# First latent step queued ahead of the second intra-chunk group, fewer late sums in the scan, direction sums on GpSimd

## Chip, core and metric

One core of a Trainium2 chip runs the whole program once. The number that counts is the device time of one execution in microseconds (us), median over the runs; lower is better. Five engines take part, each with a queue of its own that is worked off in order: TensorE (PE; its weight loads are shown apart as PEld), VectorE (DVE), ScalarE (ACT), GpSimd (POOL) and SyncE (SP), which issues the DMAs.

## What is computed

One layer of a diffusion backbone: 512 latent tokens and 256 context tokens of width 1024. The part that the change touches is the gated delta rule, run over chunks of 64 tokens, forward and backward, with the state S (64x64 for each of 8 heads) carried from chunk to chunk:

```python
def step(S, xs):
    w_c, uv_c, qd_c, intra_c, kt_c, gl_c = xs
    u = uv_c - einsum('bhck,bhkv->bhcv', w_c, S)
    o = einsum('bhck,bhkv->bhcv', qd_c, S) + einsum('bhij,bhjv->bhiv', intra_c, u)
    S = exp(gl_c)[..., None, None] * S + einsum('bhck,bhcv->bhkv', kt_c, u)
    return S, o
...
o_dc, s_cf, s_cb = bidir_delta(context, zero, zero)
o_dl, _, _ = bidir_delta(latents, s_cf, s_cb)      # o_f + flip(o_b)
y_d = rms_norm(o_dl, dn_norm_g) * silu(z)
y = sigmoid(gate_a) * (y_a @ w_br_attn) + sigmoid(gate_d) * (y_d @ w_br_dn)
x = x + gt1 * (y @ w_out);  x = x + gt2 * mlp(x, sh2, sc2)
```

Here `intra_c` is the masked product of queries and keys inside a chunk (the intra-chunk matrices). `gt1`, `sh2`, `sc2`, `gt2` are sums over a 1024x6144 matrix times a vector; the kernel forms those four as late sums, since they are needed late.

## The kernel before

**Matmuls.** Large projections are three fp32 matmuls per 128x128 weight tile (high part times high, high times low, low times high). A weight tile is fetched by DMA into one of four buffers (`wfetch`, L250, tag `wr`), its high part made by ACT (L259, `wh`) and its low part by DVE (L262, `wl`); of `wh` and `wl` there are two buffers each.

**Fill.** The scan is a chain of short steps, so other matmuls are laid between them. `filler` is a generator over the attention branch's output and the gate tiles; `gate_tiles` (L1004) yields after each 128x512 matmul, 24 to a tile. A finished tile goes through an activation (L148 is the helper's line) and for some tiles a DVE operation (L1009).

**Late sums.** `late_mod` fetches 512 KB (L1068, into the same four `wr` buffers under the name `wa`) and multiplies and sums it on DVE (L1070, 128x1024). One call of `run_late` takes one such piece, so the buffer that it uses comes back when L1070 is done.

**Intra-chunk matrices.** Two groups g = 0, 1. Of each, PE forms query-key products (`half_products`, L754, two halves), with fill before and between (`run_both`, 24 fills counting 12 before and 12 between; it takes one late sum for every `LATE` fills). DVE then multiplies by decay masks (L1254, L1255) and copies (L1261), ACT copies (L1262, L1263) and GpSimd sets zeros (L1264, L1265).

**The scan over latents.** `steps(range(NCC, NC_))` walks 8 steps; in each, both directions go through three phases. Phase one: PE forms Z from keys, queries and the state (L1128), DVE forms R (L1132, L1133). Phase two: PE forms U (L1140), DVE scales it (L1146, `uk`), ACT copies it (L1150, `us`) and scales the query part (L1152, `zq`). Phase three: PE forms the state update (L1161) and the outputs inside the chunk (L1165); ACT decays the old state (L1175) and DVE subtracts (L1177), which is the state that the next Z needs. In the first four steps DVE adds the two output parts (L1184). In the last four the other direction has already written the place: DVE adds the parts (L1187), adds the sum to what stands there (L1189), ACT squares (L1190) and DVE reduces (L1191). After the three phases 8, 7 and 3 fills are taken, and a late sum after every third.

**What sets the order.** The code only gives the order in which the operations are recorded. A list scheduler then sets each engine's queue from its own cost estimates, so an engine's order can differ from the order of the code; a queue, once set, is worked off strictly in order.

Of the kernel before, what the change touches and what calls it, by code (L numbers as in the profile page):

```python
# [12 lines left out]
ALU = mybir.AluOpType  # L13
# [13 lines left out]
WARM = 3, 6, 4, 4  # L27
NONES = 16
AHEAD = 2
LATE = 12  # L30
HPAUSE = 2
FPAUSE, CPAUSE = 12, 16
NPL = ()
# [13 lines left out]
NCC = CTX // CH  # L47
NCL = SEQ // CH
NC_ = NCC + NCL
# [50 lines left out]
def tile_layer(ctx: ExitStack, tc: tile.TileContext, I: dict, out: bass.AP, dbg=None):  # L100
    nc = tc.nc
    V, A, G, PE = nc.vector, nc.scalar, nc.gpsimd, nc.tensor
# [26 lines left out]
    def dump(key, ap):  # L129
        if dbg is not None and key in dbg:  # L130
            nc.sync.dma_start(out=dbg[key], in_=ap)
# [532 lines left out]
    for src, cols in ((abx, slice(0, SEQ)), (abc, slice(SEQ, TOK))):  # L664
        n = cols.stop - cols.start
# [433 lines left out]
    def run_both(n):  # L1099

        for _ in range(n):
            next(fill, None)
            both[0] += 1
            if both[0] % LATE == 0:
                run_late(1)
# [8 lines left out]
    def chain_step(d, step):  # L1114
# [65 lines left out]
        if lat:  # L1180
            us.free()
            dst = ot_[:, cl * 256:(cl + 1) * 256]
            if step - NCC < NCL // 2:
                V.tensor_tensor(dst, zq, oi[:, :256], op=ALU.add)  # L1184
                oi.free()
            else:
                V.tensor_tensor(zq, zq, oi[:, :256], op=ALU.add)  # L1187
                oi.free()
                V.tensor_tensor(dst, dst, zq, op=ALU.add)  # L1189
                A.activation(zq, dst, AF.Square)  # L1190
                V.tensor_reduce(oss[:, cl], hv(zq), axis=AX.X, op=ALU.add)  # L1191
            zqb.free()

    def steps(r):
        for step in r:
            both = [chain_step(d, step) for d in range(2)]
            for _ in range(3):
                for g in both:
                    next(g, None)
                yield  # L1200
# [40 lines left out]
        b.free()  # L1241

    IA = [alloc(2048, True), alloc(2048, True)]
    ia = [v64(b.ap) for b in IA]
    for g in range(2):
        ms = slice(16 * g, 16 * g + 16)
        es = slice(512 * g, 512 * g + 512)
        run_both(FILL[2] - FPAUSE)
        qq_ = bank(2)
        qD, qO = diag_off(qq_)  # L1250
        for _ in half_products(qq_, 1 + g, qT):
# [13 lines left out]
            G.memset(ia[1][lo, ms, HC:], 0.0)  # L1265
    for b in ED + [EO]:
        b.free()
    dump("kT0", kT[0].ap)
    dump("qT0", qT[0].ap)

    ot_ = alloc(2048, True)
    ot = ot_.ap.rearrange("p (c q v) -> p c q v", c=NCL, q=4)
    for n, _ in enumerate(steps(range(NCC, NC_))):
        run_fill(FILL[3][n % 3])
        if n % 3 == 2:
            run_late(1)
    for _ in fill:
        pass
# [284 lines left out]
```

## Time and profile before

| | us |
|---|---|
| median of 3 runs | 921.29 |
| lowest, highest | 921.2, 923.67 |
| the profiled execution's own time | 922.56 |
| span of the profiled execution | 920.4 |
| mean granted clock, share of full | 0.994 |

The profile is of one execution. Its span runs from the first to the last instruction; 2.16 us of its time lie outside. Its time is 1.27 us above the median. A busy share of an engine is an average over the whole program; the stretch that the change touches lies between 385 and 485 us of the span: the two groups of query-key products, then the eight steps of the latent scan, then the rest of the fill. The rows below give, for stretches and single instructions, when an engine worked, how long it stood idle, and what ended the wait.

### The profile page before, as it was taken

How to read it: one execution, taken by the hardware profiler on the slowest of the kernel's cores; microseconds unless marked ns; L12 is line 12 of the kernel's file. 1: busy time of each engine (PE TensorE's matmuls, PEld its weight loads, DVE VectorE, ACT ScalarE, POOL GpSimd, SP SyncE). 2: the span in 40 equal slices, each digit the busy share in tenths (PEclk: the TensorE clock that was granted, in tenths of full speed). 3: DMA queues.
4: the chain of work that ended last, by engine and by line, in shares of the span. 5: the costliest groups of instructions: out<-in, count | busy, mean ns of one | idle time of the engine just before them, and what ended most of it. 6: DMA issues, size and time to landing. Idle time of an engine off the chain costs nothing.

```text
span 920.4 us, 16843 instructions
## 1 busy us (share of the span) xinstructions
PE 885.5 (96%) x7082; PEld 708.7 (77%) x7082; DVE 600.8 (65%) x1029; ACT 442.7 (48%) x821; POOL 12.9 (1%) x26
## 2 busy tenths in 40 slices
PE   7999998999899999979999999999999999999998
PEld 5668767867677678767778789888888888888886
DVE  3588898997787898567766978961563245324511
ACT  5577653357568886456664444650343035213400
POOL 0000000000000001010000000000000000000000
PEclk9999998999999999999999999999999999999999
DMA  9650112110000132533324674660443224322111
GB/s 353 254 201 1 47 47 69 47 47 24 24 13 24 55 105 85 182 119 94 114 61 175 220 249 130 219 210 23 160 137 92 69 92 137 100 71 83 45 46 46
DMA packets 28443, 98.24 MB, mean 107 GB/s; under 512 B 3536, under 2 KB 4176, under 8 KB 27344
## 3 DMA queue, kind: packets, MB, share of 16 engines
q1 hardware_dynamic: 28368, 97.18, 32.2%
q8 instruction: 55, 0.90, 0.4%
q14 instruction: 20, 0.16, 0.1%
HBM read 95.07 MB, written 2.10 MB: 106 GB/s over the span
## 4 chain that ended last, share of the span: by engine, by line
PE 78%; DVE 11%; ACT 5%; DMA 3%; issue 2%; SPq 0%; DVEq 0%; ACTq 0%
PE banks L315 18%; PE banks L313 18%; PE banks L314 18%; PE banks L1004 8%; PE banks L1049 2%; DMA wa<-in_wada 2%; DVE wl L262 1%; PE banks L571 1%; PE banks L1140 1%; PE banks L577 1%; PE banks L639 1%; PE banks L1161 1%; PE banks L578 1%; DVE m L1070 1%; DMA m<-in_xT 1%
## 5 line engine op out<-in xcount | busy, mean ns | idle before, releaser
L313 PE MATMUL banks<-m,m 128*128 128x512 f32 (+1 forms) x600 | 223.5, 377 | 2.8 <-DVE m L620 1.9
L314 PE MATMUL banks<-m,m 128*128 128x512 f32 (+1 forms) x600 | 224.5, 376 | 0.1
L315 PE MATMUL banks<-m,m 128*128 128x512 f32 (+1 forms) x600 | 224.5, 376 | 0.0
L259 ACT ACTIVATE m<-wr 128x1024 fp32r<-128x1024 f32 x68 | 71.7, 1059 | 151.6 <-PE banks L314 79.0
L313 PEld LDWEIGHTS banks<-m,m 128*128 128x128 f32 x600 | 111.9, 188 | 25.4 <-ACT m L319 2.5
L314 PEld LDWEIGHTS banks<-m,m 128*128 128x128 f32 x600 | 112.5, 188 | 22.1 <-DVE m L320 1.5
L315 PEld LDWEIGHTS banks<-m,m 128*128 128x128 f32 x600 | 112.5, 188 | 21.3 <-issue 1.2
L262 DVE TENSOR_TENSOR m<-wr,m 128x1024 fp32r<-128x1024 f32 x68 | 83.1, 1224 | 66.9 <-PE banks L314 34.2
L1004 PE MATMUL banks<-m,wh 128*128 128x512 f32 x320 | 105.0, 406 | 1.6 <-issue 1.1
L313 PE MATMUL banks<-m,wh 128*128 128x512 f32 (+1 forms) x280 | 103.8, 372 | 1.5 <-DVE m L595 1.0
L315 PE MATMUL banks<-m,wl 128*128 128x512 f32 (+1 forms) x280 | 101.6, 365 | 3.1 <-DVE wl L262 3.1
L314 PE MATMUL banks<-m,wh 128*128 128x512 f32 (+1 forms) x280 | 102.6, 367 | 0.0
L1447 DVE SCALAR_TENSOR_TENSOR m<-banks,modT,m 128x512 f32<-128x512 f32 x32 | 24.0, 750 | 101.2 <-PE banks L315 101.2
L259 ACT ACTIVATE wh<-wr 128x1024 fp32r<-128x1024 f32 (+1 forms) x58 | 54.5, 940 | 46.6 <-PE banks L314 19.5
L262 DVE TENSOR_TENSOR wl<-wr,wh 128x1024 fp32r<-128x1024 f32 (+1 forms) x58 | 62.2, 1073 | 18.8 <-ACT wh L259 18.8
L1004 PEld LDWEIGHTS banks<-m,wh 128*128 128x128 f32 x320 | 58.2, 189 | 14.4 <-issue 0.9
L1004 PE MATMUL banks<-m,wl 128*128 128x512 f32 x160 | 64.5, 403 | 0.0
L315 PEld LDWEIGHTS banks<-m,wl 128*128 128x128 f32 x280 | 53.3, 192 | 11.7 <-DVE wl L262 3.9
L313 PEld LDWEIGHTS banks<-m,wh 128*128 128x128 f32 x280 | 53.6, 192 | 10.1 <-DVE m L595 1.3
L314 PEld LDWEIGHTS banks<-m,wh 128*128 128x128 f32 x280 | 53.5, 191 | 8.2 <-issue 1.0
L184 ACT ACTIVATE m<-m 128x512 fp32r<-128x512 f32 (+1 forms) x56 | 34.8, 629 | 48.6 <-DVE m L1430 21.6
L1070 DVE SCALAR_TENSOR_TENSOR m<-wa,m 128x1024 f32<-128x1024 f32 x32 | 38.9, 1222 | 19.4 <-DMA wa<-in_wada 14.4
(237 smaller groups left out, 1266.3 us busy)
## 6 DMA issues: line engine op xcount, KB each, us to landing
wr<-in_wm SPq DMA_DIRECT2D x64, 512.0 KB, 3.7
wr<-in_win SPq DMA_DIRECT2D x38, 512.0 KB, 3.6
wa<-in_wada SPq DMA_DIRECT2D x32, 512.0 KB, 4.1
m<-in_wada SPq DMA_DIRECT2D x8, 1024.0 KB, 11.7
m<-in_xT SPq DMA_DIRECT2D x8, 512.0 KB, 5.9
wr<-in_wbr SPq DMA_DIRECT2D x16, 256.0 KB, 2.6
wr<-in_wout SPq DMA_DIRECT2D x8, 512.0 KB, 4.5
out<-m SPq DMA_DIRECT2D x8, 256.0 KB, 2.0
```

Of the source, the lines that this page charges most:

```text
L184: A.activation(r32(hi), src, AF.Copy)
L259: h = A.activation(r32(hi), raw, AF.Copy)
L262: V.tensor_tensor(r32(lo), raw, hi, op=ALU.subtract)
L313: PE.matmul(acc, w[0][:, k, :], xhi, start=(start and i == 0), stop=False)
L314: PE.matmul(acc, w[0][:, k, :], xlo, start=False, stop=False)
L315: PE.matmul(acc, w[1][:, k, :], xhi, start=False, stop=(stop and i == n - 1))
L571: PE.transpose(pt[:, j * P:(j + 1) * P], probs[j][:, i * P:(i + 1) * P], ident)
L577: PE.matmul(pv.ap, v, r32(phi), start=(i == 0), stop=False)
L1004: PE.matmul(acc.ap, w[x][:, k, :], hx[k][y], start=(k == p == 0), stop=(k == KT - 1 and p == 2))
L1049: PE.matmul(pa.ap, w[x][:, j, :], r32(Q[y][:, :, j, :]), start=(j == p == 0), stop=(j == 3 and p == 2))
L1070: V.scalar_tensor_tensor(t.ap, wa, 0.5, scr.ap, op0=ALU.mult, op1=ALU.mult, accum_out=modT[:, grp, j:j + 1])
L1447: V.scalar_tensor_tensor(xn_[ct], acc.ap, modT[:, 3, ct:ct + 1], xn_[ct], op0=ALU.mult, op1=ALU.add)
```

## The change

Four edits. `LATE` goes from 12 to 8: over the two groups' 72 fills nine late sums are taken in place of six. The first phase of the first latent step (Z and R of both directions) is recorded after the second group's first fills and ahead of its query-key products; the scan then goes on from its second phase, and 8 of the scan's fills fall to after its end. In the scan a late sum is taken after every third phase of the first four steps alone, so 13 have been taken by its end where 14 had been. The add of L1189 moves from DVE (`V`) to GpSimd (`G`): eight adds of 128x256.

```diff
-LATE = 12
+LATE = 8
...
-                V.tensor_tensor(dst, dst, zq, op=ALU.add)
+                G.tensor_tensor(dst, dst, zq, op=ALU.add)
...
     IA = [alloc(2048, True), alloc(2048, True)]
+    scan = steps(range(NCC, NC_))
     ia = [v64(b.ap) for b in IA]
     for g in range(2):
...
         run_both(FILL[2] - FPAUSE)
+        if g:
+            next(scan)
         qq_ = bank(2)
         qD, qO = diag_off(qq_)
         for _ in half_products(qq_, 1 + g, qT):
...
+    ot_ = alloc(2048, True)
     dump("kT0", kT[0].ap)
     dump("qT0", qT[0].ap)
 
-    ot_ = alloc(2048, True)
-    ot = ot_.ap.rearrange("p (c q v) -> p c q v", c=NCL, q=4)
-    for n, _ in enumerate(steps(range(NCC, NC_))):
+    for n, _ in enumerate(scan, 1):
         run_fill(FILL[3][n % 3])
-        if n % 3 == 2:
+        if n % 3 == 2 and n < 3 * NCL // 2:
             run_late(1)
```

What the scheduler makes of it is shown at three places. Behind L1243 the changed kernel's lines are higher by 1 to 3 (the masks L1254 and L1255 are L1257 and L1258, the copies L1261 are L1264).

PE, before: the end of the second group's second product, and behind it the first Z (`m_80` to `m_83` are the keys, `m_181`, `m_203`, `m_218`, `m_238` the queries, `m_273` a state, `banks` accumulators).

```order
L754 MATMUL banks_64<-m_203_2197,m_81_556 32x64 x4
L754 MATMUL banks_64<-m_218_2367,m_82_557 32x64 x4
L754 MATMUL banks_64<-m_238_2573,m_83_558 32x64 x4
L1128 MATMUL banks_64<-m_273_2825,m_80_555 64x64 x2
L1128 MATMUL banks_64<-m_273_2825,m_181_1868 64x64 x2
```

PE, now: the end of the first Z (`m_275` is the other direction's state), and behind it the second group's first product.

```order
L1128 MATMUL banks_64<-m_275_2827,m_82_557 64x64 x2
L1128 MATMUL banks_64<-m_275_2827,m_218_2367 64x64 x2
L1128 MATMUL banks_64<-m_275_2827,m_83_558 64x64 x2
L1128 MATMUL banks_64<-m_275_2827,m_238_2573 64x64 x2
L754 MATMUL banks_64<-m_181_1868,m_80_555 32x64 x4
L754 MATMUL banks_64<-m_203_2197,m_81_556 32x64 x4
```

The Z of both directions moved from behind the group's two products to ahead of them; the U that follows R now stands right behind the second product, with 15 fills after it, where 13 fills stood between Z and U.

DVE, before, at the same place: the last of the second group's copies, then R, then the first `uk`.

```order
L1261 COPY m_366_3885<-m_366_3885 32x16x32
L1261 COPY m_367_3886<-m_367_3886 32x16x32
L1132 TENSOR_TENSOR m_393_4185<-banks_64,eg_737 128x256
L1132 TENSOR_TENSOR m_394_4204<-banks_64,eg_737 128x256
L1133 SCALAR_TENSOR_TENSOR m_393_4185<-m_315_3144,m_393_4185 128x256
L1133 SCALAR_TENSOR_TENSOR m_394_4204<-m_322_3217,m_394_4204 128x256
L1009 SCALAR_TENSOR_TENSOR m_325_3260<-m_395_4207,m_325_3260 128x512
L1146 TENSOR_TENSOR m_399_4232<-banks_64,eg_737 128x256
```

DVE, now: behind the first group's copies come a weight split, a late sum, a gate tile's operation, and R; then a weight split and the second group's masks and copies.

```order
L262 TENSOR_TENSOR wl_391_4062<-wr_389_4059,wh_390_4061 128x1024
L1070 SCALAR_TENSOR_TENSOR m_414_4321,modT_2818<-wa_413_4319,m_346_3489 128x1024
L1009 SCALAR_TENSOR_TENSOR m_318_3197<-m_388_4056,m_318_3197 128x512
L1132 TENSOR_TENSOR m_394_4097<-banks_64,eg_737 128x256
L1132 TENSOR_TENSOR m_395_4116<-banks_64,eg_737 128x256
L1133 SCALAR_TENSOR_TENSOR m_394_4097<-m_315_3144,m_394_4097 128x256
L1133 SCALAR_TENSOR_TENSOR m_395_4116<-m_322_3217,m_395_4116 128x256
L262 TENSOR_TENSOR wl_410_4260<-wr_408_4257,wh_409_4259 128x1024
L1257 TENSOR_TENSOR m_366_3885<-m_90_757,banks_64 128x16x32
L1257 TENSOR_TENSOR m_367_3886<-m_91_758,banks_64 128x16x32
L1258 TENSOR_TENSOR m_92_759<-m_92_759,banks_64 128x512
```

R moved from behind the second group's masks and copies to ahead of them; the first `uk` (L1146) now stands behind these, and a late sum stands ahead of R.

DVE, before, at the change from the fifth step to the sixth: new states, sums of both directions, a late sum, and R.

```order
L1177 TENSOR_TENSOR m_272_2824<-m_468_4872,banks_64 128x256
L1187 TENSOR_TENSOR m_464_4826<-m_464_4826,banks_64 128x256
L1189 TENSOR_TENSOR m_392_4168<-m_392_4168,m_464_4826 128x256
L1177 TENSOR_TENSOR m_274_2826<-m_469_4898,banks_64 128x256
L1187 TENSOR_TENSOR m_467_4843<-m_467_4843,banks_64 128x256
L1191 TENSOR_REDUCE oss_271_2823<-m_464_4826 128x4
L1189 TENSOR_TENSOR m_392_4168<-m_392_4168,m_467_4843 128x256
L1070 SCALAR_TENSOR_TENSOR m_488_5069,modT_2818<-wa_487_5067,m_346_3489 128x1024
L1191 TENSOR_REDUCE oss_271_2823<-m_467_4843 128x4
L1132 TENSOR_TENSOR m_472_4931<-banks_64,eg_737 128x256
```

DVE, now, at the same place.

```order
L1177 TENSOR_TENSOR m_272_2824<-m_474_4876,banks_64 128x256
L1187 TENSOR_TENSOR m_465_4820<-m_465_4820,banks_64 128x256
L1177 TENSOR_TENSOR m_274_2826<-m_475_4902,banks_64 128x256
L1191 TENSOR_REDUCE oss_271_2823<-m_465_4820 128x4
L1187 TENSOR_TENSOR m_468_4837<-m_468_4837,banks_64 128x256
L1132 TENSOR_TENSOR m_476_4931<-banks_64,eg_737 128x256
L1191 TENSOR_REDUCE oss_271_2823<-m_468_4837 128x4
L1133 SCALAR_TENSOR_TENSOR m_476_4931<-m_322_3217,m_476_4931 128x256
L1132 TENSOR_TENSOR m_477_4950<-banks_64,eg_737 128x256
L1133 SCALAR_TENSOR_TENSOR m_477_4950<-m_315_3144,m_477_4950 128x256
```

The two adds L1189 and the late sum are gone from DVE; each reduction L1191, which needs GpSimd's add and ACT's square, stands ahead of the second direction's add or of R's second operation. GpSimd's queue, which held only settings of zeros there, holds the eight adds behind one instruction (ISA) that the builder puts ahead of the first of them.

## Rows read from the trace of the kernel before

**Rows 1.** Page, part 1: busy time, share of the span, instructions.

```profile
PE 885.5 (96%) x7082; PEld 708.7 (77%) x7082; DVE 600.8 (65%) x1029; ACT 442.7 (48%) x821; POOL 12.9 (1%) x26
```

**Rows 2.** Windows: us; busy of PE, PEld, DVE, ACT, POOL; clock; DMA share; GB/s.

```profile
385.50:403.20 17.70, 16.03 (x305) 12.54 (x304) 10.44 (x17) 6.50 (x12) 1.44 (x2) 1.00 0.51 164
403.20:411.10 7.90, 4.42 (x85) 3.38 (x77) 6.17 (x12) 6.41 (x18) 1.48 (x2) 1.00 0.46 136
411.10:414.60 3.50, 3.11 (x38) 2.37 (x39) 2.03 (x5) 1.18 (x4) 0.00 (x0) 0.51 0.00 0
414.60:442.50 27.90, 26.74 (x602) 20.81 (x601) 19.54 (x46) 16.84 (x61) 0.00 (x0) 1.00 0.32 97
442.50:477.70 35.20, 32.90 (x678) 25.22 (x677) 26.14 (x61) 21.45 (x74) 0.00 (x0) 1.00 0.31 92
```

**Rows 3.** Waits of PE, 442.5 to 478: total us, times, longest.

```profile
PE banks L1140 <- DVE m L1133: 2.3, 4, 0.7
```

**Rows 4.** Timeline of PE and PEld: start, us, instruction, idle before and its releaser.

```profile
391.97 0.63 PE L1004 MATMUL banks<-m,wh 128*128 128x512 f32 x2
...
392.67 0.63 PE L1004 MATMUL banks<-m,wh 128*128 128x512 f32 x2
...
398.19 1.10 PE L754 MATMUL banks<-m,m 64*32 64x64 f32 x64 [1.15 <-DVE m L1255]
...
403.24 1.16 PE L1128 MATMUL banks<-m,m 64*64 64x64 f32 x64
...
411.49 1.97 PE L1140 MATMUL banks<-m,m 64*64 64x64 f32 x32 [3.88 <-DVE m L1133]
...
414.54 0.14 PEld L1161 LDWEIGHTS banks<-m,m 64*64 64x64 f32 x2 [0.65 <-ACT m L1150]
...
416.53 0.60 PEld L1128 LDWEIGHTS banks<-m,m 64*64 64x64 f32 x34 [0.37 <-DVE m L1177]
...
455.57 1.15 PE L1140 MATMUL banks<-m,m 64*64 64x64 f32 x32 [0.73 <-DVE m L1133]
```

**Rows 5.** Timeline of DVE from the first group's masks on.

```profile
395.11 1.23 DVE L1070 SCALAR_TENSOR_TENSOR m<-wa,m 128x1024 f32<-128x1024 f32 x1 [3.21 <-DMA wa<-in_wada]
...
396.26 1.28 DVE L1254 TENSOR_TENSOR m<-m,banks 128x512 f32<-128x512 f32 x2
...
402.49 1.22 DVE L262 TENSOR_TENSOR wl<-wr,wh 128x1024 fp32r<-128x1024 f32 x1 [0.39 <-ACT wh L259]
...
406.49 1.28 DVE L1254 TENSOR_TENSOR m<-m,banks 128x512 f32<-128x512 f32 x2
...
410.26 0.76 DVE L1132 TENSOR_TENSOR m<-banks,eg 128x256 f32<-128x256 f32 x2
...
411.60 0.68 DVE L1009 SCALAR_TENSOR_TENSOR m<-m,m 128x512 f32<-128x512 f32 x1
```

**Rows 6.** Timeline of ACT: copies of the second group; one square in the second half.

```profile
408.40 1.26 ACT L1262 ACTIVATE m<-m 32x512 f32<-32x512 f32 x2 [1.41 <-DVE m L1255]
...
451.86 0.40 ACT L1190 ACTIVATE m<-m 128x256 f32<-128x256 f32 x1
```

**Rows 7.** Timeline of SP's queue: the issue of a late sum's transfer.

```profile
390.19 0.33 SPq L1068 DMA_DIRECT2D wa<-in_wada  x1
```

**Rows 8.** DVE, 442.5 to 480, by line: count, busy us, mean ns.

```profile
L1070 DVE SCALAR_TENSOR_TENSOR m<-wa,m 128x1024 f32<-128x1024 f32 x4 | 4.9, 1219 | 0.1
L1189 DVE TENSOR_TENSOR m<-m,m 128x256 f32<-128x256 f32 x8 | 3.4, 422 | 0.2
```

**Rows 9.** POOL by line and form, whole span.

```profile
L1264 POOL MEMSET m<- 32x512 f32 x4 | 2.9, 730 | 26.7 <-issue 17.7 <-DVE m L1261 9.1
L1265 POOL MEMSET m<- 32x512 f32 x4 | 2.1, 516 | 5.8 <-DVE m L844 5.7
L463 POOL MEMSET m<- 64x768 f32 x2 | 1.5, 732 | 62.0 <-PE banks L210 51.3 <-PE banks L302 10.7
```

## The prediction

> **What bounds the kernel now.** I read the page's busy shares first. PE is busy for 96% of the span [rows 1], so time can come from two places only: work taken from PE, or idle time of PE. The change takes no matmul away; it can only close PE's gaps, some 35 us in all, and only those near the scan. The windows come next [rows 2]: the reader is to compare the length of each stretch with PE's busy time. From 385.5 to 403.2 PE lacks 1.7 us, from 403.2 to 411.1 3.5 us, from 411.1 to 414.6 0.4 us at half clock (0.51, the lower level of 1.2 GHz, right behind PE's longest wait here), in the scan's first half 1.2 us and in its second half 2.3 us. PE's timeline says who was waited for [rows 4]: 1.15 us ahead of the second group's product, for DVE's mask; 3.88 us ahead of the first U, for R; 0.65 us ahead of the first outputs, for ACT's copy of U. DVE's timeline says why R was late [rows 5]: R (L1132, from 410.26) stands behind the second group's masks and copies (from 406.49), and these needed a product that PE ended at about 403.2. So ahead of the scan the limit is the order of DVE's queue, and in the second half it is DVE again: its R ends all four waits, 2.3 us [rows 3].
>
> **The scan's start: what goes.** Gaps before: 1.15 + 3.88 + 0.65 = 5.68 us. The half clock made the first U 1.97 us where a later one is 1.15 [rows 4], so 0.82 more. Together 6.5 us.
>
> **The scan's start: what comes.** I rebuild both queues from the durations of before. Pitches: a fill 0.233 us (three from 391.97 to 392.67 [rows 4]) and about 0.2 us for the edges of a block (an estimate); Z, U or outputs 1.09, a product 1.03 (the rows' 1.16 and 1.10 less the 0.07 of pipeline drain, an estimate); on DVE a 1024-wide operation 1.15 (395.11 to 396.26), masks and copies of a group 3.77 (406.49 to 410.26), R of both directions 1.34 (410.26 to 411.60) [rows 5], that is 0.34 for each of its four.
> LATE 8 puts nine late sums ahead of the first group's masks where seven stood. The ninth's transfer needs a free buffer; by the releases it is issued about when the seventh was, at 390.2 [rows 7], and that one landed by 395.11, when its sum started [rows 5]. I take 394.5 for the landing (bounds 393.9 and 396), the sum until 395.7, so the masks start 0.5 us sooner than at 396.26. PE ends its fill at 397.04 (398.19 less 1.15), now does Z (to 398.1), and the product behind it finds its accumulator free since about 397.6: the gap of 1.15 is gone. Product 399.2, 12 fills 402.2, product 403.2.
> DVE: masks and copies to 399.5, weight split 400.6, the tenth late sum 401.8, a gate operation 402.4, first R at 403.4. U starts at 403.5, **gap 0.3**; it ends at 404.6, and 15 fills run to 408.3.
> DVE goes on: R to 403.8, weight split 404.9, masks and copies of the second group 408.7, then the first `uk`, ready at 409.2. The state update waits for it: **gap 0.9**. ACT's four copies of the group follow the masks (ready at about 406.8) at 0.63 each [rows 6], until 409.4, and the two copies of U with half a scaling between them end at 410.8; the second direction's outputs wait for that: **gap 1.2** with the handoffs. No gap is near 3.88, so I expect no half clock. Sum 2.4 us, so the start gains 6.5 − 2.4 = **4.1 us**. As a cross-check, the second Z comes at about 411.8 where it came at 416.53 [rows 4], with two fills fewer ahead of it. The eight fills that the scan no longer takes come behind it: PE does them either way. Its last chain on DVE and ACT has 31 fills as cover, 7.2 us, where 25 stood; if that were too short, the normalisation behind the scan would show it.
>
> **The scan's first half.** The fills now start at another place in a weight tile, so a tile's split comes ahead of the second step's copy of U on ACT and between its new states on DVE. I charge half of one 1.22 us split [rows 5]: **0.6 us lost** (bounds 0 and 1.22).
>
> **The scan's second half.** DVE loses four late sums of 1.22 and eight adds of 0.42 [rows 8], 8.2 of its 26.1 busy us [rows 2]; by that alone the 2.3 us of waiting [rows 3] would go. But a wait is added: each reduction L1191 needs GpSimd's add and then ACT's square, and it is queued ahead of the other direction's L1187 or of R (the order above). Behind it on DVE waits R, behind R PE's U. So two links DVE → GpSimd → ACT → DVE stand in series per step. GpSimd's add X has no row. The nearest ones are its settings of zeros [rows 9]: 0.516 and 0.730 for 512 elements a partition, 0.732 for 768. An add reads 2x256 and writes 256, 768 in all: I take X = 0.73. Bounds: 0.42, what DVE takes [rows 8], below and 1.1 (0.73 x 768/512) above. With the square's 0.40 [rows 6] and about 0.25 for handoffs, a link is 1.4, two are 2.8, where 2 adds and a late sum were 2.06. Step by step I get gaps of 0, 0.7, 1.35 and 0, sum 2.05 where 2.3 stood: **0.25 us gained**. Some seven links lie on the path, so X moves this by 7 times its error: +2.2 at 0.42, −2.6 at 1.1.
> By the Trainium skill (GPSIMD Engine Reference, 3.1 Elementwise), a two-input add costs GpSimd about 2.6 cycles an element at 1.2 GHz, an estimate of 0.56 us for 256 before dispatch; that would make the sum about 1.2 us better than my 0.73.
>
> **The sum.** 4.1 − 0.6 + 0.25 = 3.75 us. The profiled execution took 922.56 and would take 918.8; the median lies 1.27 lower, so 921.29 − 3.75 = **917.5 us**. What this measurement can tell from no change is about 0.3%, 2.8 us: faster is below 918.5, slower above 924.1.
>
> **Rivals.**
> (1) *Better.* GpSimd's add is as quick as DVE's (+2.2) and the copies of U are not late (half of 2.4, +1.2): 914.1. For it: the settings of zeros take 1.0 to 1.4 ns an element written, which for the add's 256 is under 0.42 [rows 9]. Against it: they read nothing, and each of them takes longer than 0.42 as a whole.
> (2) *The gain is given back once.* The first add is held up by GpSimd loading what it needs: an ISA instruction precedes it in the queue, and no add has run there. Everything from the fifth step on waits for it. For it: one queue, one first use. Against it: the instruction waits for nothing, and GpSimd has no work from 411.1 on [rows 2], while the first add is due in the second half, from 442.5, so it may be done long ahead. With all of 3.75 us given back: 921.3, no change; from 6.6 us on it would be slower.
> The Trainium skill (GPSIMD Engine Reference, 2.1 Instruction dispatch) says that the first call to a freshly loaded kernel pays an instruction load of about 6 us that no row of a profile shows; none of the rows here does. On the path that would give an estimate of 923.5.
> (3) *Slower.* Each add excludes DVE and is excluded by it. The same 32x512 setting takes 0.730 at one line and 0.516 at the next [rows 9], which something beside it must cause. If every link waits for one DVE operation (0.42) and then holds DVE's next for the add (0.73), seven links cost 7 x 1.15 = 8.05 us: 925.5. It decides the sign from 0.54 us a link, and 0.94 makes it measurable. Against it: behind L1187 stand operations with an accumulator as one input.
> The Trainium skill (SBUF — State Buffer, the text on the shared port pair) names such a lock between GpSimd reading SBUF and a DVE operation with two SBUF inputs; by that rule L1133 alone of these would be caught, and the price is at most half.
> (4) *The start doesn't gain.* The ninth late transfer lands some 4 us after 394.5; masks, products and R shift, a gap of 3 to 4 us stays with its half clock, and of 4.1 us nothing is left: 921.3. For it: DVE stood 3.21 us for such a transfer here [rows 5]. Against it: a delay of 4 us is nearly another transfer's whole 4.9, and the DMA share in the stretch is 0.51 [rows 2].
>
> **Chances.** The forecast's case 0.53, most of it (0.45) below 918.5, the rest between 918.5 and 920 by the bounds of X and of the landing; (1) 0.12; (2) and (4) together 0.20, of which I put 0.17 within 0.3% and 0.03 above; (3) 0.15. So faster 0.57, same 0.25, slower 0.18. The range reaches from below the better case, 913.5, to 924.0: it leaves out most of (3), the worst of (2), and little below.
>
> **What would show it.** Right: ahead of the first U a gap under 1 us and a clock of 1.00 in that window; the second Z near 411.8; the gap ahead of the second group's product gone; in the second half DVE's waits ended by ACT's square, and GpSimd's adds near 0.73 with PE's waits near 2 us in all. Wrong: a gap of 3 us or more ahead of U or of the first state update (the masks are still in front, or the ninth late sum came late); a half-clock window anywhere from 397 to 415; one long gap at the fifth step (rival 2); adds or links growing to 2 us and R waiting at each of the last four steps (rival 3).

## The result and the profile after

The changed kernel takes 925.88 us (median of 20 runs, 923.05 upwards) where the kernel before takes 921.29 (20 runs). The ratio is 1.0048, 95% interval 1.0037 to 1.006: slower by about half a per cent. One execution of 2202 us was disturbed, as were the profiled ones of two experiments below; the ratios leave such executions out. The forecast was 917.5, with a range up to 924.0.

The profiled execution took 928.6 us, 2.7 above the median of its kernel, where the one before lay 1.3 above its own. Its span is 926.7, which is 6.3 us longer than the one before, though the medians differ by 4.6. The page's shares hardly differ from [rows 1]:

```profile
PE 892.2 (96%) x7082; PEld 715.2 (77%) x7082; DVE 599.5 (65%) x1021; ACT 443.4 (48%) x821; POOL 18.7 (2%) x34
```

The windows of the changed kernel, by the same borders as [rows 2] (length; busy time of PE, PEld, DVE, ACT, POOL; clock; DMA share; GB/s):

```profile
385.50:403.20 17.70, 13.34 (x169) 10.35 (x169) 13.46 (x24) 5.69 (x13) 1.44 (x2) 0.90 0.68 211
403.20:411.10 7.90, 7.90 (x240) 6.40 (x238) 4.88 (x9) 4.40 (x10) 0.00 (x0) 1.00 0.46 137
411.10:414.60 3.50, 3.50 (x20) 2.75 (x15) 3.44 (x8) 1.46 (x3) 0.74 (x1) 1.00 0.40 150
414.60:442.50 27.90, 26.20 (x580) 20.20 (x582) 19.97 (x46) 18.80 (x66) 0.74 (x1) 1.00 0.28 86
442.50:477.70 35.20, 34.30 (x707) 26.57 (x698) 21.77 (x50) 22.50 (x76) 4.33 (x6) 1.00 0.13 41
```

The borders are times, so the same window holds somewhat later work now. In the second and third window the 3.5 and 0.4 us that PE lacked are gone, as forecast; in the fourth it lacks 1.7 us where it lacked 1.2, and in the fifth, most of the scan's second half, 0.9 where it lacked 2.3. But in the first window PE now lacks 4.4 us where it lacked 1.7, and its mean clock is 0.90. PE's waits over the stretch from 380 to 520 us name it (the three largest; instruction waiting, releaser: total us, times, longest):

```profile
PE banks L1004 <- ACT m L148: 4.4, 1, 4.4
PE banks L1140 <- DVE m L1133: 0.9, 2, 0.6
PE banks L1161 <- DVE m L1146: 0.6, 1, 0.6
```

The wait of 3.88 us ahead of the first U [rows 4] is gone; the first fill behind the first group's product waits 4.4 us instead, for ACT.

To see where the time went I took four landmarks that every kernel here has from PE's timeline: the first product of the first group (L754), the first transpose behind the scan, the first row-sum matmul ahead of the MLP, and the last matmul. The segments between them, in us, each from one execution:

| kernel | to the first product | product to transposes | transposes to row sums | row sums to the end |
|---|---|---|---|---|
| before | 385.55 | 98.30 | 79.61 | 352.71 |
| changed | 387.04 | 97.91 | 81.04 | 356.15 |
| difference | +1.49 | −0.39 | +1.43 | +3.44 |

The first segment runs almost the same code; the changed kernel's execution had one more stretch at half clock in it (its mean clock from 245 to 255 us is 0.83, where the kernel before has 1.00). The scan's segment is shorter by only 0.39, and the two behind it, in whose code nothing was edited, are 4.9 us longer. So two things are to be explained: why the scan's segment gained 0.4 and not 3.75, and why the program behind it became slower.

**The wait ahead of the scan.** ACT's timeline of the changed kernel at that place, the rows of DVE that it waits for, and PE's fill (start, us, engine, line, operation; idle before and its releaser):

```profile
386.58 1.23 DVE L1070 SCALAR_TENSOR_TENSOR m<-wa,m 128x1024 f32<-128x1024 f32 x1 [4.12 <-DMA wa<-in_wada]
...
388.88 1.22 DVE L1070 SCALAR_TENSOR_TENSOR m<-wa,m 128x1024 f32<-128x1024 f32 x1
```

```profile
390.14 0.82 ACT L1175 ACTIVATE m<-m,egl 128x64 f32<-128x64 f32 x3 [6.30 <-DVE m L1070]
390.87 1.04 ACT L259 ACTIVATE wh<-wr 128x1024 fp32r<-128x1024 f32 x1
391.94 0.60 ACT L148 ACTIVATE m<-banks 128x512 f32<-128x512 f32 x1
```

```profile
392.59 0.96 PE L1004 MATMUL banks<-m,wh 128*128 128x512 f32 x2 [4.36 <-ACT m L148]
```

Read from the bottom: PE's fill waits for an eviction (L148). ACT was idle for 6.30 us before that, with the eviction and a weight split standing in its queue behind a decay of the old state (L1175), and the decay waited for the third of three late sums in a row on DVE. The first of these had itself stood 4.12 us for its transfer: of ACT's 6.30 us, 2.7 passed before the first sum began and 3.6 with the three sums. The decay reads only the context's last state and a factor; what it can wait for a late sum for is, by inference, memory that the sum's scratch tile gives back. The decays belong to the first latent step, which is now recorded earlier, so the scheduler put them earlier on ACT.

**The wait ahead of the MLP.** The second place is 180 us later. DVE and ACT of the changed kernel, then PE:

```profile
567.33 1.23 DVE L1070 SCALAR_TENSOR_TENSOR m<-wa,m 128x1024 f32<-128x1024 f32 x1
...
568.48 1.22 DVE L262 TENSOR_TENSOR m<-wr,m 128x1024 fp32r<-128x1024 f32 x1
569.62 1.27 DVE L318 SCALAR_TENSOR_TENSOR m<-m,mA,m 128x256 f32<-128x256 f32 x3
```

```profile
567.10 1.05 ACT L259 ACTIVATE m<-wr 128x1024 fp32r<-128x1024 f32 x1
568.05 0.40 ACT L148 ACTIVATE m<-m 128x256 f32<-128x256 f32 x1
570.13 1.30 ACT L319 ACTIVATE m<-m,modT 128x256 fp32r<-128x256 f32 x3 [1.68 <-DVE m L318]
```

```profile
570.78 0.98 PE L313 MATMUL banks<-m,m 128*128 128x256 f32 x3 [2.33 <-ACT m L319]
```

DVE and PE at the same place in the kernel before; the matmul waited 0.31 us:

```profile
563.66 1.22 DVE L1070 SCALAR_TENSOR_TENSOR m<-wa,m 128x1024 f32<-128x1024 f32 x1 [0.27 <-PE banks L315]
...
565.16 1.28 DVE L318 SCALAR_TENSOR_TENSOR m<-m,mA,m 128x256 f32<-128x256 f32 x3
```

```profile
566.24 0.62 PE L313 MATMUL banks<-m,m 128*128 128x256 f32 x3 [0.31 <-ACT m L319]
```

A late sum stood ahead of the first modulation (L318, L319) before, too. New are a low-part split between them on DVE and a high-part split between the two steps of the normalisation (L148) on ACT. The windows show the clock at 0.83 from 570 to 580 us.

### The profile page after: what moved, and what is told of

Read it like the earlier page. It is cut to its first block, busy times and chain, and to the rows that moved or that the text cites. A ratio compares the mean times of both kernels' runs of the same rounds, so it can differ in the third digit from the quotient of the medians.

```text
span 926.7 us, 16852 instructions
## 1 busy us (share of the span) xinstructions
PE 892.2 (96%) x7082; PEld 715.2 (77%) x7082; DVE 599.5 (65%) x1021; ACT 443.4 (48%) x821; POOL 18.7 (2%) x34
## 4 chain that ended last, share of the span: by engine, by line
PE 69%; DVE 15%; issue 7%; ACT 5%; DMA 4%; SPq 0%; POOL 0%; DVEq 0%; ACTq 0%; POOLq 0%
PE banks L313 15%; PE banks L314 15%; PE banks L315 15%; PE banks L1004 9%; PE banks L1049 2%; DVE wl L262 2%; PE banks L571 1%; DVE m L185 1%; DVE m L1070 1%; DMA wa<-in_wada 1%; DMA wr<-in_wm 1%; PE banks L577 1%; PE banks L639 1%; DVE m L834 1%; DVE m L833 1%
## 5 line engine op out<-in xcount | busy, mean ns | idle before, releaser
L313 PEld LDWEIGHTS banks<-m,m 128*128 128x128 f32 x600 | 113.1, 191 | 27.8 <-issue 2.9
L314 PEld LDWEIGHTS banks<-m,m 128*128 128x128 f32 x600 | 113.7, 190 | 22.2 <-DVE m L320 1.3
L315 PEld LDWEIGHTS banks<-m,m 128*128 128x128 f32 x600 | 113.6, 190 | 21.3 <-issue 1.2
L1004 PE MATMUL banks<-m,wh 128*128 128x512 f32 x320 | 108.1, 411 | 4.4 <-ACT m L148 4.4
L184 ACT ACTIVATE m<-m 128x512 fp32r<-128x512 f32 (+1 forms) x56 | 35.2, 630 | 51.9 <-DVE m L1432 24.4
L185 DVE TENSOR_TENSOR m<-m,m 128x512 fp32r<-128x512 f32 (+1 forms) x56 | 38.3, 689 | 20.1 <-ACT m L184 19.7
```

What stands on the lines that cost most here:

```text
L184: A.activation(r32(hi), src, AF.Copy)
L185: (eng or V).tensor_tensor(r32(lo), src, hi, op=ALU.subtract)
L313: PE.matmul(acc, w[0][:, k, :], xhi, start=(start and i == 0), stop=False)
L314: PE.matmul(acc, w[0][:, k, :], xlo, start=False, stop=False)
L315: PE.matmul(acc, w[1][:, k, :], xhi, start=False, stop=(stop and i == n - 1))
L1004: PE.matmul(acc.ap, w[x][:, k, :], hx[k][y], start=(k == p == 0), stop=(k == KT - 1 and p == 2))
```

## The experiments

Each kernel is compared with the kernel before in runs on the same chip; the ratio stands with its 95% interval. The experiments ran in four groups on four chips, where the kernel before took 921.28, 921.38, 920.85 and 921.08 us, so a difference between groups is good to some tenths at best. Segments and waits are each from one execution.

**Holding the first step's decays on ACT.** The scheduler is told to keep the decays of the first latent step behind the copy of U of that step, on the same queue:

```diff
-            A.activation(us.ap, u, AF.Copy)
+            uc = A.activation(us.ap, u, AF.Copy)
...
-                    A.activation(se[:, q * HD:(q + 1) * HD], ...)
+                    sa = A.activation(se[:, q * HD:(q + 1) * HD], ...)
+                    if step == NCC:
+                        tc.add_manual_dep(sa.ins, uc.ins.name, nosync, reason="behind the copy of U")
```

> The changed kernel, with one thing more: in the first latent step the decays of the old state (L1175 of the changed kernel) are held on ACT's queue behind the copy of U; nothing else stands in another place on any engine up to the scan. In the changed kernel these decays stand ahead of a gate tile's weight split and eviction on ACT, and PE's fill waits 4.36 us there and then runs at half clock (together 5.7 us). Theory A (the decays block ACT: they wait for a late sum on DVE to give back its memory, and split and eviction stand behind them): the wait of 4.36 falls under 1.5 us, no half clock there, the median falls by 4 to 6 us, to 920 to 922. Rival B (the three late sums that stand in a row on DVE ahead of the low part's split are what PE waits for): the wait stays at 3 us or more, the median within 1.5 us of the changed kernel's 925.9.

Measured 921.6 us, ratio 1.0007 (0.9991 to 1.0022), so 4.3 us under the changed kernel. PE's timeline at the fill:

```profile
387.45 0.73 PE L1004 MATMUL banks<-m,wh 128*128 128x512 f32 x2 [0.51 <-ACT m L148]
```

The wait is 0.51 us where it was 4.36, with the three late sums where they were; the first window has its full clock again, and the scan's segment is 93.50 us. Theory A holds in that the decays block ACT, and rival B falls for this kernel; that it is memory they wait for is not shown by this.

**Late sums throughout the scan.**

```diff
-        if n % 3 == 2 and n < 3 * NCL // 2:
+        if n % 3 == 2:
```

> The changed kernel, with late sums taken throughout the scan again (17 by its end in place of 13). Theory C (four late sums fewer in the scan push the remaining ones to the front of the MLP, where a late sum and two weight splits now stand ahead of the first modulation on DVE and ACT: PE waits 2.33 us there where it waited 0.31, and a half-clock stretch follows): the wait before the first modulated matmul falls to under 0.6 us, the median falls by 2 to 4 us against the changed kernel, less 0 to 1.5 us that the late sums cost on DVE in the scan's second half. Rival D (that wait comes from the weights' transfers or from the clock, not from the late sums): it stays at 2 us and the median moves by less than 1 us or rises.

Measured 925.34, ratio 1.0043 (1.0028 to 1.0058). The last segment falls from 356.15 to 353.73 and the one before it from 81.04 to 79.85, as theory C has it. But the second half of the scan pays it back, with 38.1 us where it took 33.64 (from the start of its first Z to the start of its last output matmul): PE waits for R 3.6 us in three places there, and the clock falls to half behind one of them. The 0 to 1.5 us expected for that was too little, and the median is within the noise of the changed kernel's.

**Both together.** The two edits above.

> Both edits together: the decays held and late sums throughout the scan. If A and C are right and add up, both waits are gone and the median is 5 to 9 us below the changed kernel's, 917 to 920, so below the kernel before. If B and D are right it is within 2 us of the changed kernel. If the waits are gone but the median stays, what costs is the clock alone.

Measured 919.83, ratio 0.9987 (0.9974 to 1.0). Both waits are gone, and the median lies where it was expected: segments 94.93, 80.10 and 353.79. PE's waits of this kernel from 560 to 600 us and from 434 to 480 us:

```profile
PE banks L313 <- ACT m L319: 0.9, 2, 0.5
```

```profile
PE banks L1140 <- DVE m L1133: 3.6, 3, 1.8
```

So the decays on ACT and the limit on late sums are, between them, enough to explain that the changed kernel is slower than the one before; of the 6.0 us regained here, 4.3 come with the hold alone.

In this kernel two late sums run beside GpSimd's adds (L1191 here), which the changed kernel never has in the second half. GpSimd, DVE and PE at the first of them:

```profile
444.60 1.59 POOL L1191 TENSOR_TENSOR m<-m,m 128x256 f32<-128x256 f32 x1 [1.38 <-DVE m L1189]
```

```profile
444.38 1.22 DVE L1070 SCALAR_TENSOR_TENSOR m<-wa,m 128x1024 f32<-128x1024 f32 x1
```

```profile
448.14 1.15 PE L1140 MATMUL banks<-m,m 64*64 64x64 f32 x32 [1.81 <-DVE m L1133]
```

The add takes 1.59 us where it takes 0.74 otherwise, and ends 0.6 us after the late sum. The square, the reduction and R follow it one after another, so its delay of 0.85 us is part of PE's longest wait for R.

**The adds on DVE again.**

```diff
-                G.tensor_tensor(dst, dst, zq, op=ALU.add)
+                V.tensor_tensor(dst, dst, zq, op=ALU.add)
```

> The changed kernel with the adds of both directions on DVE again. The trace of the changed kernel shows GpSimd's add at 0.736 us, as taken in the sum, and no wait of PE for it in the second half beyond 0.6 us. By the sum (0.25 us gained with late sums gone and adds moved) the adds alone are worth little: with them on DVE and no late sums there, the median moves within 1.0 us of the changed kernel's either way. By the rival that GpSimd's links cost (seven links of 0.5 us or more) it would fall by 3 us or more.

Measured 923.8, ratio 1.0029 (1.0015 to 1.0043): 2.1 us under the changed kernel, more than the 1.0 allowed and less than the 3 of the rival. The second half, from the start of its first Z to the start of its last output matmul, takes 32.99 us where it took 33.64. (The expectations further on count only to the start of the last block of outputs: 32.1 here, 32.7 in the changed kernel, 34.15 in the kernel before.) So the move to GpSimd costs 0.65 us there. Another 1.15 us of the scan's segment is a shorter wait at the first fill, 3.21 us in this execution, which the adds don't touch.

**The first latent step early, alone.** The kernel before with `scan = steps(...)` and `next(scan)` alone; LATE, adds and late sums as before.

```diff
+    scan = steps(range(NCC, NC_))
...
+        if g:
+            next(scan)
...
-    for n, _ in enumerate(steps(range(NCC, NC_))):
+    for n, _ in enumerate(scan, 1):
```

> The kernel before with one part alone: the first latent step's first phase ahead of the second group's products (LATE 12, adds on DVE, late sums throughout the scan). On ACT all eight decays of the first step now stand ahead of the gate tile's weight split and eviction. Theory A (ACT's decays wait for a late sum's memory) expects PE's wait at the fill after the first product here too, 2 to 5 us with a half-clock stretch, against 4 to 5 us gained at the scan's start: median 919 to 923. Rival B (the wait comes from LATE 8's three late sums in a row on DVE) expects no wait there and the whole gain: 915.5 to 918.

Measured 922.74, ratio 1.0011 (0.9997 to 1.0025). The median lies where theory A had it, but see the next. PE's times in its trace can't be set beside the others; the order on ACT and DVE can be read:

```profile
435.73 2.03 ACT L1175 ACTIVATE m<-m,egl 128x64 f32<-128x64 f32 x8
439.75 1.06 ACT L259 ACTIVATE wh<-wr 128x1024 fp32r<-128x1024 f32 x1 [2.00 <-PE banks L1004]
```

```profile
434.41 1.22 DVE L1070 SCALAR_TENSOR_TENSOR m<-wa,m 128x1024 f32<-128x1024 f32 x1
...
438.37 1.23 DVE L1070 SCALAR_TENSOR_TENSOR m<-wa,m 128x1024 f32<-128x1024 f32 x1 [2.73 <-DMA wa<-in_wada]
```

Here too the decays stand ahead of the split, but all eight run without a wait that shows, ahead of the late sum that stands for its transfer.

**The same with the decays held.**

> The same, with the first step's decays held on ACT's queue behind the copy of U. Theory A: no wait at the fill, the first two steps' gaps fall from 6.5 to about 2.5 us, nothing else moves: median 916 to 918.5, 2.5 to 5 us under the run without the hold. Rival B: the same as without the hold.

Measured 923.54, ratio 1.0022 (1.0013 to 1.0032). Neither theory had this. The scan's segment is 93.91 us, 4.4 under the kernel before, as hoped. But the segment behind it is 85.57 where it was 79.61. PE and SP there (L1340 are the loads of x):

```profile
528.34 0.50 PE L313 MATMUL banks<-m,wh 128*128 128x512 f32 x1 [2.83 <-ACT wh L259]
```

```profile
516.35 1.76 SPq L1340 DMA_DIRECT2D m<-in_xT  x4
```

PE waits 2.83 us for a weight tile of the output projection. Four loads of x, which the kernel before issued between 493.5 and 499.7, are issued at 516 among the projection's weight loads. The run without the hold issues its loads of x just as late in the order of the queue. That the hold made nothing better, and that the decays ran without a wait there, narrows theory A: with LATE 12 the early decays cost nothing that can be measured; it took the late sums of LATE 8 as well.

**LATE 8 alone.**

```diff
-LATE = 12
+LATE = 8
```

> The kernel before with LATE 8 alone: nine late sums ahead of the first group's masks where seven stood, the scan's first phase where it was. The decays stay behind the copies on ACT. Theory A: no wait over 1.5 us at the fill; the masks move by 1 us at most; median within 1.5 us of before, 920 to 923. Rival B: the wait of 3 us or more at the fill after the first product, median 924 or more.

Measured 923.97, ratio 1.0026 (1.0013 to 1.0039). The fill waits 0.5 us, so rival B falls again. The first masks come 1.5 us sooner after the first product (9.2 us for 10.7), but R still stands behind the second group's masks: PE waits 4.3 us for it where it waited 3.9, and the stretch at half clock behind that is longer. Alone, LATE 8 loses, by 1 us more than the 1.5 that theory A allowed.

**The limit on late sums alone.**

```diff
-        if n % 3 == 2:
+        if n % 3 == 2 and n < 3 * NCL // 2:
```

> The kernel before with the late sums in the scan's first half alone (10 in place of 14 by the scan's end). From the runs so far: the second half, from its first Z to its last outputs, shortens by about 2 us (32.1 where 34.15 stood), and from the scan's end on the program lengthens by 2 to 5 us (1.3 up to the MLP and up to 3.5 at its start, by theory C). Median 921 to 925. Rival D (the MLP's start is late for another reason): 919 to 920.

Measured 922.86, ratio 1.0013 (0.9998 to 1.0029). Segments 92.87, 81.66 and 355.09: the scan gains, though without the half clock of before in this execution, and the program behind it gives back 2.0 and 2.4 us. The size is as expected, the place is not theory C's: 1.6 of the 2.0 is one wait of PE for a weight's low part at 556 us, and of the 2.4 only 0.4 is at the first modulation (a wait of 0.73 us for 0.31), 0.9 a wait at 615 us for an ACT operation (L184).

**Three late sums behind the scan, adds on DVE, decays held.** From the changed kernel, with the hold and DVE's adds:

```diff
-    for _ in fill:
-        pass
+    for n, _ in enumerate(fill, 1):
+        if n % 8 == 0:
+            run_late(1)
```

> The changed kernel with three things more: the first step's decays held on ACT, the adds of both directions on DVE, and a late sum after every eighth fill behind the scan (three, so 16 are taken before the last weight products of the scan's stage). By the segments measured so far: from the first group's first product to the transposes behind the scan 92 to 94 us (98.3 before, 97.9 changed); from there to the row sums ahead of the MLP 80 to 81; from these to the end about 353.8 as in the kernels with late sums throughout, not 356 as in those with the limit. Median 917 to 919.5. If the late sums are not what makes the MLP late, the last segment stays at 355 to 356.5 and the median at 920 or more.

Measured 923.13, ratio 1.0031 (1.0019 to 1.0042). The scan's segment is 92.85 and the last one 353.03, both as expected, but the one between them 84.39: x is issued at 517.7, and the projection waits 2.5 us for a weight tile. The expectation missed that segment.

**The same with the adds on GpSimd.**

> The same with the adds on GpSimd. In the traces so far the scan's second half took 32.1 us with the adds on DVE and 32.7 with them on GpSimd where no late sums stand in it. So 0.3 to 1.0 us above the run with the adds on DVE. If GpSimd's adds cost nothing, the same within 0.3 us in the segment.

Measured 925.5, ratio 1.0057 (1.004 to 1.0073), 2.4 us more than with DVE's adds and more than the 1.0 expected. The second half takes 35.66 us where it took 33.96 (to the start of the last output matmul). One late sum fell beside an add again (1.57 us), and once DVE was the one to be late: its L1133 began 0.23 us after an add and took twice as long as the next one.

```profile
466.11 0.73 POOL L1191 TENSOR_TENSOR m<-m,m 128x256 f32<-128x256 f32 x1 [1.71 <-DVE m L1189]
```

```profile
466.34 0.79 DVE L1133 SCALAR_TENSOR_TENSOR m<-m,m 128x256 f32<-128x256 f32 x1
...
467.71 0.41 DVE L1133 SCALAR_TENSOR_TENSOR m<-m,m 128x256 f32<-128x256 f32 x1
```

**Decays held, late sums throughout, adds on DVE.**

> The changed kernel with the decays held, late sums throughout the scan, and the adds on DVE: the third run of the first series (919.83) with DVE's adds. The second half took 35.66 us there with the adds on GpSimd and 34.15 in the kernel before, with late sums and adds on DVE. So the segment from the first product to the transposes is 1 to 2 us shorter than there (93 to 94 us where it was 94.9), the rest as there; median 918 to 919.5. If GpSimd relieves DVE, it is longer than there.

Measured 918.98, ratio 0.9978 (0.9966 to 0.9989): faster than both kernels, than the one before by 0.2%. Against the same kernel with GpSimd's adds (0.9987) the medians don't separate, since the intervals overlap; the second half takes 34.7 us where it took 36.6. Segments 93.93, 79.97 and 353.57. PE's wait for R in the second half of this kernel, to be set against the 3.6 us with GpSimd's adds:

```profile
PE banks L1140 <- DVE m L1133: 1.4, 3, 0.9
```

**LATE 12, decays held, otherwise the changed kernel.**

> The changed kernel with LATE 12 again and the first step's decays held. Against the run with the decays held alone (921.6) it tells what LATE 8 is worth once ACT is free: two late sums fewer ahead of the first masks. The segment from the first product to the transposes 93 to 95 us (93.5 there); one late sum more is left for the MLP, so the last segment is 356 us or more. Median 921 to 923.5.

Measured 923.83, ratio 1.0026 (1.0013 to 1.0039). The scan's segment is the shortest of all, 91.79, but x is issued at 515.3, the projection waits 2.5 us and the segment is 85.15. So the run doesn't tell what LATE 8 is worth. The last one is 353.41, not the 356 expected, with the limit in place, and PE waits 1.0 us ahead of the MLP. In the traces that wait goes with what stands between the last sums of squares and the modulation: 2.2 to 2.3 us with a late sum and a split on DVE and a split inside the normalisation on ACT (the changed kernel, with the hold, with DVE's adds), 1.0 here with a late sum and a split on DVE alone, 1.1 with two late sums (the last run below), 0.3 to 0.4 with one (the kernel before, and the two runs with three late sums behind the scan). So it isn't the number of late sums that makes the MLP late, but how many of them and of the splits the scheduler puts at this place; theory C is right on the place and wrong on the count.

**x loaded early, on the scan part alone with the decays held.**

```diff
+    X1 = alloc(8 * SEQ, True)
+    for k2 in range(4):
+        nc.sync.dma_start(out=X1[:, k2 * 1024:(k2 + 1) * 1024], in_=I["xT"][k2])
     Y = [alloc(1024) for _ in range(8)]
...
-    X1 = alloc(8 * SEQ, True)
-    for k2 in range(4):
-        nc.sync.dma_start(out=X1[:, k2 * 1024:(k2 + 1) * 1024], in_=I["xT"][k2])
```

> The run of the scan part alone with the decays held (LATE 12, adds on DVE, late sums throughout), and one thing more: the four 512 KB loads of x, which the output projection's residual needs, are given their memory ahead of the branch products, so that they are issued early. In that run they were issued at 516 to 518 us among the projection's weight loads, and PE waited 2.8 us for a weight tile there; from the transposes behind the scan to the row sums it took 85.6 us where the kernel before took 79.6. Theory E (the late load of x makes that wait): the segment falls to 79.5 to 81 us, the wait is gone, the median falls from 923.5 to 917 to 919. Rival F (the shorter scan only meets the weight transfers sooner, whatever x does): the wait of over 2 us and a segment of 84 us or more stay, median 922 or more.

Measured 918.92, ratio 0.9974 (0.9961 to 0.9986), 4.6 us under the same kernel without this edit (1.0022 on another chip). SP issues the loads early,

```profile
493.93 1.75 SPq L1323 DMA_DIRECT2D m<-in_xT  x4
```

PE's wait for the weight tile is gone, and the segments are 93.74, 80.16 and 353.12. Theory E holds, rival F falls.

**The same with the limit.**

> The same with late sums in the scan's first half alone. The scan's segment is 91 to 92.5 us (second half without late sums, 32 us). Theory E with C (fewer late sums in the scan make the MLP late): the segment up to the row sums 80 to 82 us, from there to the end 355 to 356.5: median 917.5 to 920. If the MLP's lateness hangs on the order of the queue and not on the number of late sums (one late sum and no weight split now stand ahead of its first modulation), the last segment is 353 to 354 and the median 915.5 to 917.5.

Measured 919.66, ratio 0.9989 (0.9974 to 1.0005). No segments can be given for it; the median says only that the limit brings nothing on top.

**x loaded early in the kernel before.**

> The kernel before with the early load of x alone. There x was issued at 493 to 500 already. Theory E: nothing to gain, median within 1 us of before. If it gains 2 us or more, the gain of the two runs beside it is not the scan's.

Measured 923.11, ratio 1.0017 (1.0002 to 1.0032). The edit hardly moves the load here (494.7 to 496.0 for 493.5 to 499.7). It gains nothing, rather the reverse, so the gain beside it is the scan's, once x no longer comes late.

## Why the prediction was wrong

**The scan's start was right in its mechanism and near in size.** From the first fill behind the first product to the second Z the changed kernel takes 417.84 − 392.59 = 25.25 us, of which half clock behind the wait is about 1.55 (its fills lag those of before by that much more at 396 us than at 392.6); the kernel before took 416.53 − 387.16 = 29.37. The forecast was 4.1 us of gaps and two fills (0.5) fewer: 4.6, against 4.1 with that half clock in it and 5.7 without. The gap ahead of U was forecast at 0.3 and is none; ahead of the state update 0.9 and 0.63; for ACT's copies 1.2, and no wait above 0.24 us shows there. No half clock stood from 397 to 415 us, as called; the second Z came at 417.84 and not near 411.8. GpSimd's add was taken at 0.73:

```profile
L1189 POOL TENSOR_TENSOR m<-m,m x8: 727/739/742, 451.6 to 478.4; 128x256 f32<-128x256 f32 x8
```

(min, median and max in ns.) The first half lost about 1.3 us where 0.6 was charged: from the second Z to the fifth it took 25.89 us, 25.97 before, but with 48 fills where 54 stood, and six fills are 1.4 us by the 0.233 of the prediction. These six come behind the scan, where the last output matmul and the transposes stand 1.31 us further apart; they cost no wait. The second half, with 69 fills in both, gained 1.44 us (33.64 for 35.08) where 0.25 was forecast. The scan's segment is the sum: −3.94 (the wait below) + 4.12 + 0.08 + 1.44 − 1.31 = 0.39.

**What failed is the step "ahead of the scan".** The prediction rebuilt PE's and DVE's queues there and took ACT's from the copies on. It never followed the decays L1175 on ACT, although they belong to the step that was moved; "PE ends its fill at 397.04" took for granted that everything up to there stays. Z, forecast at 11.5 us behind the first product, came 16.9 behind it. That is 3.9 us of wait more between the first product and the first fill behind it (5.55 us for 1.61) and about 1.5 us of half clock, together about all of the 5.7 gained behind it. None of the four rivals had this wait. With the decays held, the whole changed kernel is 4.3 us faster, back at the time of the kernel before. That this takes LATE 8 too is shown by the runs with LATE 12, held and not (923.54 and 922.74), which don't differ in that direction, and by the order in the trace of the latter; LATE 8 alone, with the decays where they were, had no such wait either (0.5 us).

**What was left out is the program behind the scan.** The prediction counted late sums (13 for 14) and said of the one that moves only that PE does the fills either way. What the edit re-dealt is the order at the front of the MLP, where two splits now stand with a late sum ahead of the modulation. The last segment is 3.44 us longer for it: about 2.0 of wait (2.33 for 0.31) and about 1.7 of half clock behind it (10 us at a mean clock of 0.83). Once late sums run through the scan again it is 2.4 us less (353.73 and 353.79 for 356.15 and, with the hold, 356.55).

**In the second half the gain is the late sums', not GpSimd's.** The prediction put late sums and adds into one term: 2.3 us of waiting gone, 2.05 added by the links over GpSimd and ACT. PE's waits there came to 0.8 us, so the links were priced too high. But the run with DVE's adds shows the parts: without the late sums and with DVE's adds the second half gains 2.09 us (32.99 for 35.08; 33.4 in the run of the limit alone), and the adds on GpSimd take 0.65 of it back. Of three pairs that differ in the adds alone, DVE's are ahead in the second half by 0.65, 1.7 and 1.9 us, and in the median by 2.1, 2.4 and 0.9, the last within the noise. The price of the add was right where it runs alone; DVE was not short of 0.42 us, and the reduction behind GpSimd and ACT holds up R in DVE's queue, most where late sums stand there too (3.6 us of waits for 1.4) and make an add take 1.59.

**The rivals.** Rival 2 fell: GpSimd's set-up ran 36 us ahead of the first add, at 415.4, and the first add took 0.74 as the others.

```profile
L1189 POOLq MODIFY_POOL_CONFIG  x2: 2/2/2, 415.4 to 415.4; - x2
```

So the Trainium skill's load of about 6 us (GPSIMD Engine Reference, 2.1 Instruction dispatch) cost nothing that the trace shows, if there was one. The estimate of 0.56 us for the add before dispatch, from the Trainium skill's 2.6 cycles an element (GPSIMD Engine Reference, 3.1 Elementwise), stands beside 0.739 here. Rival 3's exclusion exists, but not in the changed kernel: there no late sum and no L1133 ran beside an add, the DVE operations that did have an accumulator as input or are reductions, and they took 0.41 to 0.42 us as elsewhere. In the runs where a late sum or L1133, both with two inputs outside the accumulators, met an add, the later of the two was held up (1.59 for 0.74, 0.79 for 0.41). So it was not seven links of 1.15 us. Rival 4's place was right, a late sum's transfer and ACT behind it, but the masks were late by 2.6 us (398.86 for 396.26 [rows 5], 1.5 of it the later start), and no gap ahead of U came of it.

**What stays open.** Why ACT's decay waits for a late sum is inferred from the releaser and from the lack of any other need; the memory itself was not tried, nor why the transfer of the first of the three sums landed as late as it did. Why x's loads get their memory late in five of the kernels was not followed further than that giving it to them early removes the wait. The last segment of the changed kernel and its like is explained by the order in the two queues, which no run held fixed by itself; that it is what piles up there, and not the number of late sums left, is read from comparing traces. Segments from single executions vary: the two runs of the unchanged scan, with x as before and early, differ by 1.0 us in the scan's segment and 1.2 in the last.

## What to carry to other kernels

When a piece of code is recorded earlier, follow every instruction of it on every queue: whatever can start early is moved up with it, and an instruction with nothing urgent to do can stand at the head of a queue and wait for another engine. In a program whose orders a scheduler sets, an edit at one place also re-deals the loads and splits far behind it: cut the trace into segments by landmarks and compare them all before a term of the sum is believed. An engine's spare time was no gain here, where the result has to come back through a second engine into a queue that something urgent stands in.

## What the runs showed of the hardware

GpSimd's add of two 128x256 fp32 tiles took 0.739 us where DVE's took 0.42 [rows 8], and no first use was dearer. Five adds in three runs started while DVE worked on a late sum, and took 1.57 to 1.59 us; one DVE operation (L1133) that started during an add took 0.79 us for 0.41. Waits of PE of 2.33, 3.88 and 4.36 us had a stretch at half clock at their end, but a wait of 3.0 us in the run of the limit alone had none; of two waits of 2.45 us for the same projection's weight tile one had it (LATE 12, decays held), the other not (three late sums behind the scan, adds on DVE). Executions differ in such stretches in the same code, too: ahead of the first product the profile of the kernel before has one, from 140 to 150 us, and that of the changed kernel three, from 60 to 80, 140 to 150 and 245 to 255, by the windows' mean clock. Two profiles can so differ by 1.5 us before the change is reached, and segments compare where spans don't.
